# One ScalarE transfer per row of softmax sums, sums laid out by head, and another order in the last head pair

## The chip, the cores and the metric

The kernel runs on one core of a Trainium2 chip. A core has five engines with queues of their own, each strictly in order: TensorE (PE; its weight loads are shown as PEld), VectorE (DVE), ScalarE (ACT), GpSimd (POOL) and SyncE (SP), which only issues transfers here. Sixteen DMA engines carry out what SP, ACT and POOL issue. The metric is device time in microseconds (us) of one execution, lower is better.

## The reference, cut to what matters

One layer (sequence 1024, width 1024) runs two branches on the same normed input, a Mamba-2 scan and a forgetting attention with 16 heads of 64, and merges them by gates. The change touches the attention branch alone:

```python
for blk in range(seqlen // ATT_BLOCK):
    s = einsum('bhqd,bhkd->bhqk', q[:, :, q0:q1], k[:, :, :q1]) * scale
    s = s + fcum[:, :, q0:q1, None] - fcum[:, :, None, :q1]
    s = where(kpos <= qpos, s, -inf)
    prob = softmax(s, axis=-1)
    outs.append(einsum('bhqk,bhkd->bhqd', prob, v[:, :, :q1]))
...
y_att = o * silu(z_att)
merged = sigmoid(g_ssm) * (y_ssm @ w_branch_ssm) + sigmoid(g_att) * (y_att @ w_branch_att)
out = merged @ w_out;  x = x + rmsnorm(out)
```

All data is float32. The kernel computes large matrix products as sums of products of rounded parts ("h" and "l" tiles), and by a block scheme with seven products (steps 1 to 7 of a `Pair`) over sums and differences of operand blocks.

## The kernel before, in words

**Two strands of work.** `Stream` is the list of all projection steps, each a (pair of output units, one of seven products). It is pumped in halves (`stream.half`), in between the work of the stage that runs beside it. First come the input projections, then with the scan beside them, then with the attention beside them; at the end the stream runs alone through the second branch product (`wba`) and the output product (`merged`).

**The attention stage** (L1288 to L1640) loops over m = 0 to 48. A head pair hp (two heads, side by side on 64 partitions each) takes six values of m, its groups g = 0 to 5 (`GROUPS`, L1310): two blocks of 128 queries against one half of the keys. The groups (7,6), (5,4) need both key halves; (3,2) and (1,0) need one. In a group, `scores` multiplies q by k, adds the forget sums on DVE with a running minimum (`ex`, `nm`, L1459), takes the exponential on ACT with its row sum (`ex`, `sm`, L1463); `turned` transposes the result on PE (`pt`) and copies it out (`p`, L1483 on ACT, L1481 on DVE); in the next value of m `weighted` multiplies by v (`av`, L1494).

**Sums.** A head pair has three rows of results, n = 0, 1, 2, each 512 numbers wide per head, which end after g = 1, 3 and 5 (`end`). For n = 0 and 1 a row holds both key halves h of 256 queries; for n = 2 it holds the four blocks of g = 4 and 5. `settle` finds the common minimum of the two halves and exp of the differences; `scale` makes the factors `ns` (128 queries x 8); `send` turns them on PE into 8 rows x 128 (`tp`), copies them on ACT (`st`, L1385) and writes them to DRAM (`st_dram`, L1387, POOL, two transfers of 4 rows). `take` reads them back spread over 64 partitions per head (`rb`, L1393, two transfers on SP), and `out` multiplies the unnormed result by them (L1424 or L1418, DVE), adds the two halves (`zr`, L1425), and hands the row on through `outputs`.

**Order in one m.** Products of the former group; `free` (result times gate, L1412); scores; `stream.release()`; `settle` of the row that ends here; `take` (or, for rows 1 and 2 of the last head pair, `out`) of the row that ended at m - 2; some halves of the stream; `scale`; loads for later groups; `turned`; `out` at m - 2; `send` of the row that ended at m - 1; more halves. At the end of each m the stream's work on operand pieces is held back (`hold`), and `release` lets it go: `Operands.some` fetches pieces of the next branch product's operands (SP, L265) and splits pieces that have landed (ACT L277/L280, then DVE L278/L281, tiles x0 to x6).

**The last head pair.** For hp = 7 the finished rows don't go through DRAM: `out(1)` (at m = 47) makes with L1526 and L1527 the last pieces of the operands -t2 (x4), t3 (x5) and -b22 (x2), and `out(2)` (at m = 48) those of b21 (x1) and t4 (x6), through `put` and `direct`. The stream's step in the attention's last stretch, (wba 0, 6), reads -t2; steps 7 (t3), 1 of the next pair, 2 (b21), 4 (t4) and 3 (-b22) follow.

**What sets the order on an engine.** A planner sorts each engine's instructions by readiness in its own simulated time and by program order; `pin` ties an instruction behind the one written just before it on the same engine, and `high_priority` moves one forward. All matrix products, the transposes, the score work and the splits are pinned; `rb` loads, piece fetches and `settle`/`scale` aren't. The send's transfer is pinned, on POOL behind POOL's last instruction.

Of the kernel before, what the change touches and what calls it, by code (L numbers as in the profile page):

```python
# [12 lines left out]
ALU = mybir.AluOpType  # L13
# [3 lines left out]
P = 128  # L17
# [69 lines left out]
def hybrid_layer(ctx: ExitStack, tc, a, out):  # L87

    nc = tc.nc
# [42 lines left out]
    def turn(out_, in_, idn=ident):  # L132
        return tc.keep_in_program_order(nc.tensor.transpose(out_, in_, idn))  # L133

    def pin(op):
        return tc.keep_in_program_order(op)
# [1151 lines left out]
    with tc.tile_pool(name="att", bufs=1, reuse_waits="tile", side="right") as ap, tc.tile_pool(  # L1288
# [45 lines left out]
        class Heads:  # L1334
# [10 lines left out]
            def at(self, t, i, h, e):  # L1345

                if i < 4:
                    return t[2][:, i // 2, e, i % 2 : i % 2 + 1]
                return t[(7 - i) // 2][:, h, e, i % 2 : i % 2 + 1]

            def settle(self, n):

                if n == 2:
                    return
                nr = ap.tile([P, 2, 2], F32, tag="nr", name="nr")
                dd = self.dd[n] = ap.tile([P, 2, 2, 2], F32, tag="dd", name="dd")
                nm = self.nm[n]
                nc.vector.tensor_tensor(nr, nm[:, 0], nm[:, 1], ALU.min)
                for h in range(2):
                    nc.vector.tensor_tensor(dd[:, h], nr, nm[:, h], ALU.subtract)  # L1360
                nc.scalar.activation(dd, dd, AF.Exp)

            def scale(self, n):

                sm = self.sm[n]
                ns = self.ns[n] = ap.tile([P, 2, 2, 2], F32, tag="ns", name="ns")
                if n == 2:
                    nc.vector.reciprocal(sm, sm)
                    nc.vector.tensor_scalar(ns, sm, 0.5, None, ALU.mult)
                    return  # L1370
                dd = self.dd[n]
                nc.vector.tensor_tensor(sm, sm, dd, ALU.mult)
                nc.vector.tensor_tensor(sm[:, 0], sm[:, 0], sm[:, 1], ALU.add)
                nc.vector.reciprocal(sm[:, 0], sm[:, 0])
                flat = [x.rearrange("p h e t -> p h (e t)") for x in (ns, dd, sm)]
                over = flat[2][:, 0:1, :].to_broadcast([P, 2, 4])
                nc.vector.scalar_tensor_tensor(flat[0], flat[1], 0.5, over, ALU.mult, ALU.mult)

            def send(self, n):

                tp = pp.tile([P, HALF], F32, tag="s", bufs=4, name="tp")
                turn(tp[0:8, 0:P], self.ns[n].rearrange("p h e t -> p (h e t)"))
                st = small("st")[0:8, 0:P]
                with tc.high_priority():
                    nc.scalar.activation(st, tp[0:8, 0:P], AF.Copy)  # L1385
                for h in range(2):
                    pin(nc.gpsimd.dma_start(st_dram[self.hp, n, :, 256 * h : 256 * h + 256], st[4 * h : 4 * h + 4, :]))  # L1387

            def take(self, n):

# [181 lines left out]
        def end(m):  # L1572

            hp, g = divmod(m, 6)
            if 0 <= hp < NK and g % 2:
                yield heads[hp], g // 2
# [15 lines left out]
        def fill(m, part):  # L1592
            share = weights[min(m // 6, NK - 1)] * rooms[m % 6][part]
            to = stream.steps.index((ends[4], 6))
            stream.halves(round((2 * (to - stream.at) - (stream.run is not None)) * share / left[0]))
            left[0] -= share

        made = []
        for m in range(6 * NK + 1):

            for one in made:
                weighted(*one)
            for hd, which in end(m - 1):
                hd.free(which)
            if m == 6 * NK:
                stream.release()
                heads[NK - 1].out(2)
                break
            hp, g = divmod(m, 6)
            if not g:  # L1610
                heads[hp] = Heads(hp)
            for u in range(2):
                scores(hp, g, u)
            stream.release()
            for hd, which in end(m):
                hd.settle(which)
            for hd, which in end(m - 2):
                if not hd.last or not which:
                    hd.take(which)
                else:  # L1620
                    hd.out(which)
            fill(m, 0)

            for hd, which in end(m):
                hd.scale(which)
                hd.load_gates(which)
            loads(m)
            made = turned(hp, g)
            for hd, which in end(m - 2):
                if not hd.last or not which:  # L1630
                    hd.out(which)
            for hd, which in end(m - 1):
                hd.send(which)
            if m == 6 * NK - 1:
                heads[hp].send(2)
            stream.hold()
            fill(m, 1)
            for hd, which in end(m if m == 6 * NK - 1 else m - 1):
                if hd.last and which:
                    hd.take(which)  # L1640
# [59 lines left out]
```

## Time and profile before

| | us |
|---|---|
| median of 3 runs | 1342.09 (1340.25 to 1342.15) |
| profiled execution | 1341.3 |
| its span, first to last instruction | 1339.6 |
| PE busy | 1277.4 (95%) |
| DVE busy | 1017.7 (76%) |
| ACT busy | 787.0 (59%) |
| POOL busy | 307.4 (23%) |
| attention stage in that span | about 720 to 1185 |
| mean granted clock of PE | 0.986 |

The profile gives each instruction its start, its length and the idle time of its engine before it, with the event that ended that idle time ("<-"). A line such as `L1424 ... o<-o,rb` names the line of the kernel, the tiles written and read, and `x16` the number of instructions. Stretches are in microseconds from the span's start. The granted clock is what PE was given in a stretch, as a share of full speed; matmul ends are modelled, so a busy PE may still run at half speed. DMA issues have the time in which the issuing engine's queue is held and, apart from it, the time to landing.

### The profile page before, as it was taken

Reading aid. Unit: us, or ns where it says so; the run is one execution under the profiler, and the core shown is the slowest. Engines: PE = TensorE matmul, PEld = TensorE weight load, DVE = VectorE, ACT = ScalarE, POOL = GpSimd, SP = SyncE. Lnnn points to the kernel's source line nnn. Section 1 sums busy time; section 2 is a strip of 40 time slices with the busy share of each in tenths; the row PEclk is TensorE's granted clock in tenths of the full one; section 3 lists DMA queues with packets and bytes.
Section 4 is the critical chain, followed back from the end, with each engine's and each line's share of the span. In section 5 each row is a group of like instructions: output and inputs, shape, how many; then the busy total and the mean of one; then the engine's idle time right before and its main releaser. Section 6 shows DMA issues by size and latency. Waiting matters only on the chain.

```text
span 1339.6 us, 21075 instructions
## 1 busy us (share of the span) xinstructions
PE 1277.4 (95%) x7070; PEld 995.5 (74%) x7070; DVE 1017.7 (76%) x1978; ACT 787.0 (59%) x1726; POOL 307.4 (23%) x311
## 2 busy tenths in 40 slices
PE   6899999999999999999999999999889998889997
PEld 4578878777887888878877777777567766568786
DVE  7878986886888888888676576667676667776875
ACT  7645665465665666576556665556665555543664
POOL 4000340013400340034001122231111213235152
PEclk9999999999999999999999999999899998989999
DMA  8133542545436543654374556576765567556933
GB/s 286 59 105 79 163 143 100 176 161 164 123 114 205 174 118 115 200 179 129 125 279 150 168 201 204 185 232 222 264 215 192 192 200 239 186 158 193 355 121 102
DMA packets 154668, 233.59 MB, mean 174 GB/s; under 512 B 17216, under 2 KB 62656, under 8 KB 154560
## 3 DMA queue, kind: packets, MB, share of 16 engines
q1 hardware_dynamic: 142016, 205.53, 47.9%
q0 software_dynamic: 6400, 16.10, 3.2%
q10 hardware_dynamic: 6144, 10.62, 2.1%
q8 instruction: 55, 0.90, 0.3%
q14 instruction: 53, 0.43, 0.1%
HBM read 162.99 MB, written 72.34 MB: 176 GB/s over the span
## 4 chain that ended last, share of the span: by engine, by line
PE 60%; DMA 13%; DVE 11%; ACT 9%; issue 4%; SPq 1%; POOL 1%; ACTq 0%; DVEq 0%; POOLq 0%
PE pb L130 26%; PE pc L130 15%; PE pd L130 5%; PE av L130 3%; PE s L130 3%; ACT ex L1463 3%; PE pt L133 2%; PE yps L130 2%; DVE wop L352 2%; DVE ex L1459 1%; DMA raw<-in_wu 1%; ACT wop L351 1%; DMA st_dram<-st 1%; DMA rb<-st_dram 1%; PE tr L133 1%
## 5 line engine op out<-in xcount | busy, mean ns | idle before, releaser
L1463 ACT ACTIVATE ex<-ex,nm 128x512 f32<-128x512 f32 (+1 forms) x192 | 116.0, 606 | 149.7 <-DVE nm L1459 147.7
L352 DVE TENSOR_TENSOR wop<-sum,wop 128x512 fp32r<-128x512 f32 x180 | 139.2, 774 | 55.8 <-ACT wop L351 54.4
L351 ACT ACTIVATE wop<-sum 128x512 fp32r<-128x512 f32 x180 | 112.4, 625 | 81.6 <-DVE sum L357 30.3
L352 DVE TENSOR_TENSOR wop<-raw,wop 128x512 fp32r<-128x512 f32 x144 | 112.0, 779 | 45.2 <-ACT wop L351 41.6
L404 ACT ACTIVATE s<-pb 128x512 f32<-128x512 f32 x144 | 84.9, 590 | 89.6 <-PE pb L130 88.3
L130 PE MATMUL pc<-x3h,wop 128*128 128x512 f32 x384 | 132.2, 402 | 2.0 <-DVE th L418 1.2
L130 PE MATMUL pc<-x2h,wop 128*128 128x512 f32 x384 | 130.8, 399 | 3.0 <-DVE th L416 3.0
L130 PE MATMUL pb<-x4h,wop 128*128 128x512 f32 x384 | 130.4, 397 | 2.1 <-ACT x4h L277 2.1
L130 PE MATMUL pb<-x0h,wop 128*128 128x512 f32 x384 | 132.2, 401 | 0.0
L130 PE MATMUL pb<-x5h,wop 128*128 128x512 f32 x384 | 130.6, 399 | 1.5 <-ACT s L404 1.5
L130 PE MATMUL pb<-x6h,wop 128*128 128x512 f32 x384 | 130.0, 397 | 0.5 <-ACT s L404 0.5
L1459 DVE CUSTOM_DVE_ANT_0 ex<-s,fb 128x512 f32<-128x512 f32 (+1 forms) x192 | 95.7, 551 | 36.2 <-PE s L130 36.1
L133 PE MATMUL pt<-ident,ex 128*128 128x128 f32 x576 | 83.2, 287 | 16.4 <-ACT ex L1463 15.7
L130 PE MATMUL pd<-x1h,wop 128*128 128x512 f32 x288 | 96.6, 394 | 0.0
L351 ACT ACTIVATE wop<-raw 128x512 fp32r<-128x512 f32 x144 | 89.5, 622 | 11.7 <-PE pc L130 5.2
L133 PEld LDWEIGHTS pt<-ident,ex 128*128 128x128 f32 x576 | 69.2, 146 | 32.0 <-ACT ex L1463 25.7
L130 PEld LDWEIGHTS pc<-x3h,wop 128*128 128x128 f32 x384 | 73.1, 190 | 20.9 <-issue 2.6
L130 PEld LDWEIGHTS pc<-x2h,wop 128*128 128x128 f32 x384 | 72.1, 188 | 21.1 <-DVE th L416 4.3
L130 PEld LDWEIGHTS pb<-x5h,wop 128*128 128x128 f32 x384 | 73.1, 190 | 19.2 <-ACT s L404 2.7
L130 PEld LDWEIGHTS pb<-x4h,wop 128*128 128x128 f32 x384 | 72.3, 188 | 18.6 <-ACT x4h L277 2.5
L130 PEld LDWEIGHTS pb<-x0h,wop 128*128 128x128 f32 x384 | 73.3, 191 | 16.1 <-issue 0.7
L130 PEld LDWEIGHTS pb<-x6h,wop 128*128 128x128 f32 x384 | 72.7, 189 | 16.8 <-ACT s L404 0.9
(308 smaller groups left out, 2971.2 us busy)
## 6 DMA issues: line engine op xcount, KB each, us to landing
raw<-in_wu SPq DMA_DIRECT2D x128, 256.0 KB, 3.9
csb<-cs_dram SPq DMA_DIRECT2D x32, 256.0 KB, 5.3
fb<-f_dram SPq DMA_DIRECT2D x16, 512.0 KB, 6.6
rb<-st_dram SPq DMA_DIRECT2D x48, 128.0 KB, 3.0
wd<-in_wo SPq DMA_DIRECT2D x40, 128.0 KB, 3.0
xt<-in_x SPq DMA_DIRECT2D x8, 512.0 KB, 5.8
gs_dram<-th ACTq DMA_DIRECT2D x16, 256.0 KB, 3.5
qh_dram<-th SPq DMA_DIRECT2D x16, 256.0 KB, 2.9
```

The costliest lines, as they stand in the source:

```text
L130: return tc.keep_in_program_order(nc.tensor.matmul(*args, **kw))
L133: return tc.keep_in_program_order(nc.tensor.transpose(out_, in_, idn))
L351: nc.scalar.activation(op[:, 0], src, AF.Copy)
L352: nc.vector.tensor_tensor(op[:, 1], src, op[:, 0], ALU.subtract)
L404: nc.scalar.activation(s, ps, AF.Copy)
L1459: nc.vector.tensor_tensor_reduce(o, s[e][:, 0:w], fb[hp, h][:, e, 0:w], 1.0, 3.0e38, ALU.add, ALU.min, nm)
L1463: pin(nc.scalar.activation(o, o, AF.Exp, scale=-1.0, bias=nm, accum_out=hd.at(hd.sm, i, h, e)))
```

## The change

Three edits in the attention stage. (1) `send` issues one transfer of 8 rows from ScalarE's queue, right behind the copy it sends and moved forward by the planner with it, in place of two of 4 rows from GpSimd's. (2) So that the 8 rows lie in DRAM order (head, half, block), the tiles `nm`, `sm`, `dd` and `ns` are indexed head first, half second; the division in `scale`, one DVE instruction over both halves until now, becomes one for each half, since the sum over halves no longer broadcasts in one flattened operand. (3) In the loop, `take` (for the last head pair's rows 1 and 2 `out`) stands ahead of `stream.release()` and `settle`.

```diff
@@ class Heads
             def at(self, t, i, h, e):
                 if i < 4:
-                    return t[2][:, i // 2, e, i % 2 : i % 2 + 1]
-                return t[(7 - i) // 2][:, h, e, i % 2 : i % 2 + 1]
+                    return t[2][:, e, i // 2, i % 2 : i % 2 + 1]
+                return t[(7 - i) // 2][:, e, h, i % 2 : i % 2 + 1]
 ...
-                nc.vector.tensor_tensor(nr, nm[:, 0], nm[:, 1], ALU.min)
+                nc.vector.tensor_tensor(nr, nm[:, :, 0], nm[:, :, 1], ALU.min)
                 for h in range(2):
-                    nc.vector.tensor_tensor(dd[:, h], nr, nm[:, h], ALU.subtract)
+                    nc.vector.tensor_tensor(dd[:, :, h], nr, nm[:, :, h], ALU.subtract)
 ...
-                nc.vector.tensor_tensor(sm[:, 0], sm[:, 0], sm[:, 1], ALU.add)
-                nc.vector.reciprocal(sm[:, 0], sm[:, 0])
-                flat = [x.rearrange("p h e t -> p h (e t)") for x in (ns, dd, sm)]
-                over = flat[2][:, 0:1, :].to_broadcast([P, 2, 4])
-                nc.vector.scalar_tensor_tensor(flat[0], flat[1], 0.5, over, ALU.mult, ALU.mult)
+                total = sm[:, :, 0]
+                nc.vector.tensor_tensor(total, total, sm[:, :, 1], ALU.add)
+                nc.vector.reciprocal(total, total)
+                for h in range(2):
+                    nc.vector.scalar_tensor_tensor(ns[:, :, h], dd[:, :, h], 0.5, total, ALU.mult, ALU.mult)
 ...
-                turn(tp[0:8, 0:P], self.ns[n].rearrange("p h e t -> p (h e t)"))
+                turn(tp[0:8, 0:P], self.ns[n].rearrange("p e h t -> p (e h t)"))
                 st = small("st")[0:8, 0:P]
                 with tc.high_priority():
                     nc.scalar.activation(st, tp[0:8, 0:P], AF.Copy)
-                for h in range(2):
-                    pin(nc.gpsimd.dma_start(st_dram[self.hp, n, :, 256 * h : 256 * h + 256], st[4 * h : 4 * h + 4, :]))
+                    pin(nc.scalar.dma_start(st_dram[self.hp, n].rearrange("e (r c) -> (e r) c", r=4), st))
@@ the loop over m
             for u in range(2):
                 scores(hp, g, u)
-            stream.release()
-            for hd, which in end(m):
-                hd.settle(which)
             for hd, which in end(m - 2):
                 if not hd.last or not which:
                     hd.take(which)
                 else:
                     hd.out(which)
+            stream.release()
+            for hd, which in end(m):
+                hd.settle(which)
             fill(m, 0)
```

## The prediction

> **What bounds the kernel now.** I read the page first, then busy time by stretches, the waits, the chain of work around single sends, and the instructions in order of time at four places.
>
> ```profile
> span 1339.6 us, 21075 instructions
> ...
> 720.00:1185.00 465.00, 434.83 (x2864) 320.10 (x2861) 317.29 (x809) 276.29 (x711) 104.27 (x140) 0.97 0.63 206
> 959.67:963.08 3.41, 0.23 (x1) 0.14 (x1) 3.41 (x9) 0.95 (x4) 1.81 (x2) 1.00 0.24 50
> 963.08:969.91 6.83, 6.58 (x23) 4.12 (x24) 3.37 (x10) 4.39 (x13) 1.14 (x2) 0.50 0.76 257
> 1000.63:1004.04 3.41, 1.61 (x7) 0.73 (x5) 3.41 (x9) 1.77 (x5) 2.84 (x4) 1.00 0.99 308
> 1004.04:1010.87 6.83, 6.19 (x21) 4.67 (x23) 3.83 (x8) 3.18 (x9) 1.68 (x3) 0.50 0.52 193
> 1116.68:1120.09 3.41, 2.09 (x8) 0.98 (x6) 2.23 (x9) 2.65 (x8) 3.31 (x5) 1.00 0.88 299
> 1120.09:1126.92 6.83, 5.71 (x20) 4.50 (x22) 1.67 (x3) 2.96 (x8) 1.55 (x3) 0.50 0.63 204
> 1154.23:1157.64 3.41, 1.75 (x17) 1.06 (x16) 3.06 (x6) 3.10 (x7) 0.00 (x0) 1.00 0.84 262
> 1157.64:1161.05 3.41, 3.41 (x29) 2.44 (x28) 3.41 (x6) 0.00 (x0) 1.28 (x1) 1.00 0.33 114
> 1178.12:1181.53 3.41, 1.36 (x7) 0.81 (x5) 3.27 (x5) 0.71 (x2) 1.40 (x2) 1.00 0.28 41
> 1181.53:1188.36 6.83, 5.99 (x13) 3.91 (x14) 5.42 (x9) 4.18 (x8) 0.00 (x0) 0.50 0.89 287
> ```
>
> A stretch's columns are its length, then PE, PEld, DVE, ACT and POOL busy with instruction counts, the granted clock, the DMA share and GB/s. **TensorE is the bound**: in the attention stage (720 to 1185) it is busy 434.83 of 465, so only 30.2 us of idle time can come back directly. There is a second price. After the stretch at 959.67, in which PE worked 0.23 of 3.41 us, the clock is 0.50 for 6.83 us; likewise after 1.80 us of idle (1000.63), 1.32 (1116.68) and 2.05 (1178.12). After 1.66 us (1154.23) it stays at 1.00. So a stretch with some 1.3 to 1.8 us of idle can cost the next one half its speed: up to half of PE's 5.7 to 6.6 us there, some 3 us each. Short waits of PE are what this change can be worth, together with the clock they cost.
>
> The waits that the change aims at, and one send in full (the chain of waits):
>
> ```profile
> DVE o L1424 <- DMA rb<-st_dram: 7.3, 6, 2.3
> SPq L1393 <- DMA st_dram<-st: 101.8, 25, 8.3
> ...
> 989.91 0.15 ACT st L1385
> 990.34 0.54 POOL st_dram L1387
> 990.88 2.75 DMA st_dram<-st
> 994.27 3.15 DMA rb<-st_dram
> ...
> 997.51 0.69 DVE L1424 TENSOR_TENSOR o<-o,rb 128x512 f32<-128x512 f32 x1 [2.33 <-DMA rb<-st_dram]
> 954.87 0.69 DVE L1418 TENSOR_TENSOR zr<-o,rb 128x512 f32<-128x512 f32 x1 [1.89 <-DMA rb<-st_dram]
> 1154.58 0.69 DVE L1424 TENSOR_TENSOR o<-o,rb 128x512 f32<-128x512 f32 x1 [1.59 <-DMA rb<-st_dram]
> ```
>
> ACT copies the row of sums out (done at 990.06), POOL issues two transfers one behind the other, the second lands 2.75 us after its issue began, SP, which stood waiting for it, issues the broadcast `rb`, and DVE stands 2.33 us because its queue is in order and `o` is at its head. SP spends 101.8 us of the stage at this wait, but PE feels only what DVE passes on.
>
> **The change, part by part.** First the send (L1386 to L1387). The rows that price it:
>
> ```profile
> L1387 POOL DMA_DIRECT2D st_dram<-st x48: 547/572/584, 725.1 to 1177.1; - x48
> DMA to landing us min/median/max: 1.6/2.7/5.9
> L621 ACTq DMA_DIRECT2D gs_dram<-th x16: 326/327/355, 41.6 to 810.7; - x16
> 228.86 0.33 SPq L993 DMA_DIRECT2D rr_dram<-row  x1
> 230.57 0.81 SPq L996 DMA_DIRECT2D r<-rr_dram  x2
> 1148.21 0.72 ACT L1463 ACTIVATE ex<-ex,nm 128x512 f32<-128x512 f32 x1 [2.49 <-DVE nm L1459]
> ```
>
> Now the second transfer begins its issue 990.88 - 990.06 = 0.82 us after the copy ends. ScalarE issues behind its own instruction; I take that as immediate, so one issue of 0.33 us replaces a hop and two of 0.57. The landing itself I take as unchanged: the nearest transfer of the new shape, the 8 rows of 512 B that SP writes at 228.86, lets its reader go 1.71 us later, against 1.6 us for POOL's quietest. So **0.8 us earlier per send**. Bounds: nothing, where the write waits for other traffic (median 2.7 against 1.6) rather than for its issue; and 0.8 + (2.7 - 1.7) = 1.8 us if the single write also escapes that traffic.
>
> *The Trainium skill ("DMA: Bandwidth & Descriptors", Issuing engines are not separate DMA queues) says that transfers issued from another engine still run on the same 16 DMA engines and save only the time to initiate them. By that rule the 0.8 us is all there is, and the upper bound of 1.8 falls away; the 1.71 beside 1.6 us agrees.*
>
> What 0.8 us buys, place by place:
> - At 997.51 DVE starts 0.8 us earlier, PE's idle in the stretch at 1000.63 falls from 1.80 to 1.0. That is 0.8 us, and if the clock then holds, half of PE's 6.19 us, 3.1 more. An idle of 1.0 lies below every stretch quoted that lost the clock, but DVE's queue can refill it; I count the clock at 0.6. Term 2.7, ends 0 and 3.9.
> - At 954.87 DVE runs full through 963.08 (3.41 of 3.41), so 0.8 us comes through; PE still idles over 2 us, the clock falls anyway. Term 0.8, ends 0 and 1.8.
> - At 1154.58 the two issues stood behind another transfer on POOL, and PE's later pause is 1.48 us (row below). Term 1.0, ends 0 and 1.48.
> - The rest of the 7.3 us is in shorter waits. DVE has idle time elsewhere (317.29 busy of 465), so I give them no term.
>
> What it costs on ScalarE: 24 x 0.33 = 7.9 us. In its cover is the idle time in which ScalarE waits for the next scores: 2.49 us at 1148.21, the first instruction behind a copy `st` there. If that cover were gone, all 7.9 us would lie before `ex` and thus before PE's transposes. POOL is freed of 48 x 0.572 = 27 us; its remaining stores and differences come earlier, which I price at nothing.
>
> **Layout by head** (L1347 to L1377). Only the division is split:
>
> ```profile
> L1360 DVE TENSOR_TENSOR dd<-nr,nm 128x4 f32<-128x4 f32 x30 | 3.5, 158 | 0.4
> 1164.64 0.16 DVE L1377 SCALAR_TENSOR_TENSOR ns<-dd,sm 128x8 f32<-128x8 f32 x1
> 1167.70 0.27 PE L133 MATMUL tp<-ident,ns 128*8 128x128 f32 x1 [0.39 <-DVE p L1481]
> ```
>
> Sixteen instructions become 32 of four columns, by the first row 0.158 us each: at most 16 x 0.158 = 2.5 us more on DVE. `ns` is done 2.9 us before PE wants it even in the last pair, so only the length of DVE's queue counts, and only where DVE is full, as at 959.67. I charge 0.9 us for this and for the one or two places where ScalarE has no gap; ends 0 and 2.5 + 0.7.
>
> **The order at the start of a group** (L1614 to L1621). For every pair, SP's two `rb` loads now come ahead of the fetches of operand pieces that `release` emits, and the pieces' splits come ahead of `settle`. Queued behind SP's wait are then those pieces and the next q, k and v; the wait has been up to 8.3 us, but what stands behind the wait gets away when the row has landed, and that comes 0.8 us earlier than now. Term 0; the ends are a gain of 0.8 and, for pieces that went ahead until now, a loss of the wait itself, some 101.8 / 25 = 4 us of lateness, which PE feels only if its next step reads them. It bites in the last group (m = 47), where `out(1)` goes ahead of the splits:
>
> ```profile
> 1175.07 0.61 ACT L280 ACTIVATE x6h<-x6l 128x512 fp32r<-128x512 f32 x1
> 1175.59 0.57 ACT L1483 ACTIVATE p<-pt 128x512 f32<-128x512 f32 x1
> 1180.73 0.63 ACT L277 ACTIVATE x4h<-x 128x512 fp32r<-128x512 f32 x1 [4.41 <-DVE x L1526]
> ...
> 1175.10 0.68 DVE L278 SCALAR_TENSOR_TENSOR x2l<-x2l,x2h 128x512 fp32r<-128x512 f32 x1
> 1177.04 0.68 DVE L281 TENSOR_TENSOR x6l<-x6l,x6h 128x512 fp32r<-128x512 f32 x1
> 1180.01 0.68 DVE L1526 TENSOR_TENSOR x<-zr,x 128x512 f32<-128x512 f32 x1
> ...
> 1163.99 0.33 PE L133 MATMUL pt<-ident,ex 128*128 128x128 f32 x1 [1.48 <-ACT ex L1463]
> 1176.21 0.87 PE L130 MATMUL av<-p,v 128*64 128x256 f32 x8 [1.32 <-ACT p L1483]
> 1181.41 0.70 PE L130 MATMUL pb<-x4h,wop 128*128 128x512 f32 x1 [2.05 <-ACT x4h L277]
> ```
>
> PE stands 2.05 us for the last piece of -t2, which comes out of `out(1)` through `x`. Two splits (x2l, x6l) lie before `x` on DVE, 0.6 us apart each from the next instruction: without them `x4h` and PE's matmul come 1.2 us earlier. On ScalarE x6h no longer precedes `p`, 0.52 us off the 1.32. PE's idle in the stretch at 1178.12 then is about 2.05 - 1.2 + 0.5 = 1.35 us, between the cases that lost the clock and the one that kept it; I count half of 5.99, 3.0, at two thirds. Term 1.2 + 2.0 = 3.2, ends 0 (the planner or a late `rb` keeps `x` where it is) and 2.05 + 0.52 + 3.0 = 5.6. Late next are the moved pieces, x2 and x6; the steps that read them come after three others.
>
> **Sum**: 2.7 + 0.8 + 1.0 + 3.2 - 0.9 = 6.8 us. The profiled execution took 1341.3 us, 1.7 beyond its span; 1341.3 - 6.8 = 1334.5. The median of the runs shown, 1342.09, is 0.8 above it, so the forecast is **1335.3 us**.
>
> **The rivals.**
> - *Hidden anyway.* The 0.8 us per send disappears in traffic, and the planner, which orders what isn't pinned, shifts other DVE and ACT work so that pauses come up elsewhere. For: SP's 101.8 us shows that few of these waits reach PE; the clock fell after 1.32 us at 1116.68, a place that `rb` doesn't touch, and one new such place costs 1.3 + 2.9 = 4.2. Time: 1342.1 - 6.8 + 4.2 = 1339.5, and 1341.7 with half of the send's 4.5 us gone as well.
> - *Only the idle time returns.* The clock terms, 0.6 x 3.1 = 1.9 and 2.0, fail: PE's pauses shrink, but those stretches stay at 0.50, or others take their place. Time: 1335.3 + 3.9 = 1339.2. For it: 1.32 us lost the clock and 1.66 didn't, so a shorter pause is no warrant. *The Trainium skill ("TensorE: Matmul & The Clock Gate", What's actually happening) puts the half-rate state behind at least one idle window of about 3.4 us; by that rule no trimming of a 1.8 us pause wins clock, and the time would be this one. The trace differs: the stretch at 1000.63 had 1.61 us of matmuls in it and the clock fell all the same.*
> - *All pauses close.* Every term at its far end: 3.9 + 1.8 + 1.5 + 5.6 = 12.8, less 0.4: 1329.7; with the pause before 963.08 closed far enough to keep the clock (half of 6.58, 3.3) 1326. Against it: DVE is full at those places.
> - *Slower: ScalarE's queue stands.* ScalarE is in order, so when its transfer must wait for a free place behind an unrelated transfer, `ex` and `p` wait too, where POOL's wait held up nothing that PE needs. For it:
>
> ```profile
> ACT ex L1463 <- DMA ga_dram<-th: 1.9, 1, 1.9
> ```
>
>   one such wait of 1.9 us in this stage, on ScalarE. Against: it is one, and ScalarE issues gate transfers already (the row of 16 above). Price: the cover is about 2.5 us, so it decides where a wait passes 2.5 us or where a split or `p` follows at once. Three such places, each 1.9 us and one lost clock of 3, cost 8.7, against what is left of the gains in the tail, 3.2: 1342.1 + 5.5 = 1347.6.
>
> **How the numbers follow.** Forecast, 1329 to 1338: 0.41. Only idle, around 1339: 0.12. All closed, below 1329: 0.11. Hidden, within 2.7 us (0.2%, about what a measurement of this kernel can tell from no change) of 1342.1: 0.20. ScalarE's queue, above 1344.8: 0.16. So faster 0.64, same 0.20, slower 0.16. The range 1327 to 1346 leaves out some 0.06 below and 0.13 above.
>
> **What would show it.** Right: one ACT-queue issue of about 0.33 us per send and a transfer landing 1.6 to 3 us behind it; SP's wait for `st_dram` down by some 20 us; DVE's 7.3 us before `o` at less than half; the stretches after 1004 and 1181 at clock 1.00; PE's wait for `x4h` below 1.4 us. Wrong: ACT rows with waits for DMAs before `ex`; `x2l` and `x6l` still ahead of `x`; an unchanged or larger wait for `rb`; or new stretches at clock 0.50 in other pairs.

## The result, and the profile after

The changed kernel takes 1325.68 us (median of 7 runs, 1320.04 to 1333.79), the kernel before on the same chip 1340.25 (7 runs, 1336.59 to 1350.31): a ratio of **0.9887, 95% interval 0.9859 to 0.9914**, some 15 us less. The forecast was 1335.3. The runs of one kernel lie several us apart and go with the clock that PE was granted: of the changed kernel's seven, the one at 0.989 took 1333.79 us and the one at 0.995 took 1320.04.

The page of the changed kernel, its busy times, two of its queues (q0 is GpSimd's, q10 ScalarE's, by what the change moved) and the chain that ended last:

```profile
span 1325.7 us, 20994 instructions
...
PE 1268.7 (96%) x7070; PEld 990.7 (75%) x7070; DVE 1020.0 (77%) x1994; ACT 786.2 (59%) x1726; POOL 278.6 (21%) x263
...
q0 software_dynamic: 4864, 15.99, 3.2%
q10 hardware_dynamic: 6528, 10.72, 2.1%
...
PE 67%; DVE 10%; DMA 9%; ACT 9%; issue 3%; SPq 1%; POOL 1%; ACTq 0%; DVEq 0%; POOLq 0%
```

DVE, ACT and POOL changed by what was forecast: 16 more instructions on DVE, 48 fewer on POOL and 29 us less there. PE runs the same 7070 matmuls in the same order as before, so the two traces can be laid on each other matmul by matmul. How far the changed kernel is ahead at the start of a matmul, summed up by place (times of the kernel before):

```
stretch of the kernel before      us gained there   what PE's rows show
to 720, ahead of the stage        -2.4              +1.6 a clock fall at 55, -4.0 longer waits
720 to 900, short pauses          +3.0              up to 0.62 each before pt, tp and av, shorter or gone
937 pause for ex                  -0.8              0.93 -> 1.75
939 to 946                        -0.8              half clock for 6.8 us, was 3.4
963 pause for ex                  +2.5              3.88 -> 1.43
966 to 970                        +1.1              half clock for 3.4 us, was 6.8
970 to 1060, short pauses         +1.8              0.3 to 0.5 each before pt, gone
1003 pause for ex                 -1.4              1.38 -> 2.76
1004 to 1011                      +1.0              half clock for 3.4 us, was 6.8
1095 pause for p                  +1.3              1.45 -> 0.17
1119 to 1127                      +1.0              half clock for 3.4 us, was 6.8
1164 pause for ex                 +1.6              1.48 -> 0
1174 to 1181 tail, pauses         +2.2              tp 1.35 longer; av 1.32, x4h 2.05 gone
1181 to 1188 tail, clock          +3.0              half clock, now full
between these and behind          +0.8
sum                               13.9              spans 1339.6 and 1325.7
```

Ahead of 720 no instruction of the change runs, and the profiled executions of the experiments below lie between 3.4 us behind the kernel before and 2.2 ahead of it there, so the 2.4 us are what executions differ by. From 720 on the changed kernel gains 16.3 us: 5.3 are matmuls that ran at a better clock (1.1 + 1.0 + 1.0 + 3.0 - 0.8), and the other 11.0 are shorter pauses and what lies around them. The stage, and the stretches around the falls of the clock from 959 on, in the changed kernel (columns as before: length, PE, PEld, DVE, ACT, POOL busy, granted clock, DMA share, GB/s):

```profile
720.00:1185.00 465.00, 442.73 (x2946) 329.60 (x2943) 329.63 (x841) 282.14 (x722) 78.18 (x93) 0.98 0.63 210
...
959.20:962.61 3.41, 1.59 (x7) 0.73 (x5) 3.41 (x14) 1.89 (x8) 0.56 (x1) 1.00 0.65 163
962.61:969.44 6.83, 6.83 (x34) 4.72 (x35) 3.59 (x10) 4.04 (x10) 0.00 (x0) 0.75 0.76 239
1000.16:1003.57 3.41, 1.16 (x5) 0.59 (x6) 3.38 (x11) 3.06 (x9) 0.00 (x0) 1.00 0.63 235
1003.57:1010.40 6.83, 6.83 (x42) 5.37 (x43) 2.16 (x4) 1.81 (x5) 0.54 (x1) 0.75 0.21 74
1116.21:1123.04 6.83, 6.83 (x42) 5.19 (x41) 3.49 (x5) 2.57 (x6) 1.36 (x1) 0.75 0.50 157
1167.40:1170.80 3.40, 2.82 (x17) 2.08 (x18) 3.40 (x8) 2.25 (x6) 0.00 (x0) 1.00 0.01 1
1170.80:1177.60 6.80, 6.07 (x27) 4.71 (x26) 6.19 (x9) 4.03 (x8) 1.30 (x1) 1.00 0.74 243
```

The clock still falls after 962.61, 1003.57 and 1116.21, but the mean over 6.83 us is 0.75 where it was 0.50; in the tail it stays at 1.00. At 939 it went the other way: 0.50 over 6.82 us, where in the kernel before it came back after 3.41.

The waits of the changed kernel in the stage that the change aims at, and the same send as in the prediction:

```profile
SPq L1392 <- DMA st_dram<-st: 94.3, 21, 7.7
...
DVE o L1423 <- DMA rb<-st_dram: 4.2, 5, 2.0
...
986.72 0.25 ACT L1385 ACTIVATE st<-tp 8x128 f32<-8x128 f32 x1
987.00 0.29 ACTq L1386 DMA_DIRECT2D st_dram<-st  x1
988.29 1.59 SPq L1392 DMA_DIRECT2D rb<-st_dram  x2
994.08 0.69 DVE L1423 TENSOR_TENSOR o<-o,rb 128x512 f32<-128x512 f32 x1 [2.04 <-DMA rb<-st_dram]
```

From the end of the copy (986.97) to SP's `rb` it is 1.32 us; before it was 993.77 - 990.05 = 3.72. But `rb` itself now needs 5.79 us from its issue to DVE's start, against 3.74 before, so at this place nearly all of it was given back: DVE stands 2.04 us where it stood 2.33. Over all 24 sends, the mean from copy's end to SP's issue went from 4.15 to 2.76 us, and DVE stood 4.8 us in all before `o` or `zr`, against 10.8.

### The profile page after: what moved, and what is told of

Same layout as the page of the kernel before. It is cut to its first block, busy times and chain, and to the rows that moved or that the text cites. A ratio compares the mean times of both kernels' runs of the same rounds, so it can differ in the third digit from the quotient of the medians.

```text
span 1325.7 us, 20994 instructions
## 1 busy us (share of the span) xinstructions
PE 1268.7 (96%) x7070; PEld 990.7 (75%) x7070; DVE 1020.0 (77%) x1994; ACT 786.2 (59%) x1726; POOL 278.6 (21%) x263
## 3 DMA queue, kind: packets, MB, share of 16 engines
q0 software_dynamic: 4864, 15.99, 3.2%
## 4 chain that ended last, share of the span: by engine, by line
PE 67%; DVE 10%; DMA 9%; ACT 9%; issue 3%; SPq 1%; POOL 1%; ACTq 0%; DVEq 0%; POOLq 0%
PE pb L130 29%; PE pc L130 16%; PE pd L130 5%; PE av L130 4%; PE s L130 4%; PE pt L133 4%; ACT ex L1462 2%; PE yps L130 2%; DVE wop L352 2%; DMA raw<-in_wu 2%; ACT wop L351 1%; PE tr L133 1%; DMA xt<-in_x 1%; DVE ex L1458 1%; DVE sum L357 1%
## 5 line engine op out<-in xcount | busy, mean ns | idle before, releaser
L351 ACT ACTIVATE wop<-raw 128x512 fp32r<-128x512 f32 x144 | 89.5, 622 | 10.9 <-PE pc L130 5.0
L133 PE MATMUL pt<-ident,ex 128*128 128x128 f32 x576 | 80.4, 284 | 13.4 <-ACT ex L1462 13.0
```

Source lines behind the costliest of these rows:

```text
L351: nc.scalar.activation(op[:, 0], src, AF.Copy)
```

## The experiments

Two readings recur below, both from the profiled execution of each kernel: **L**, the mean over the 24 sends from the copy's end to the issue of `rb` on SP (4.15 before, 2.76 changed), and **D**, DVE's idle time ahead of the instructions `o` and `zr` that read `rb` (10.8 and 4.8). Ratios are to the kernel before on the same chip, with 95% intervals.

### The two halves of the change

The changed kernel with the old order in the loop (`send_only`), and the kernel before with only the new order (`order_only`):

```diff
 # send_only: the transfer and the layout of the change, but
             stream.release()
             for hd, which in end(m):
                 hd.settle(which)
             for hd, which in end(m - 2):   # take / out
 # order_only: L1387 and the layout of before, but
             for hd, which in end(m - 2):   # take / out
             stream.release()
             for hd, which in end(m):
                 hd.settle(which)
```

> The changed kernel with the loop's old order: one ScalarE transfer per row and the layout by head, but release and settle ahead of take and out. Theory A (the rows arrive earlier, everywhere): SP's rb loads follow the copy by some 2.8 us instead of 4.1, the gain is about 9 of the 15 us of the whole change, 0.6 to 0.7% under the kernel before, and the last group keeps its pause before x4h and a half-rate stretch after it. Theory B (the order in the last group gives nearly all): within 0.2% of the kernel before.

> The kernel before with the new order alone: take and out ahead of release and settle; two GpSimd transfers, old layout. Theory A: only the last group gains, 4 to 6 us (0.3 to 0.45%): PE's 2.05 us before x4h shrink to under 1.4 and the clock stays at 1.00 after it; TensorE's other pauses as before. Theory B: 12 us or more (0.9%).

`send_only` 0.9932 (0.9905 to 0.9958), L 2.64, D 1.5. `order_only` **1.0025 (1.0003 to 1.0046)**, L 4.14, D 12.8. The send alone brings most of the gain; the order alone, expected to bring 4 to 6 us, brings none. The execution profiled was its fastest (1335.39 us, median 1341.30), so the loss isn't in it, but its tail shows why nothing is won there, by DVE's and PE's instructions in order of time and two stretches:

```profile
1169.30 0.69 DVE L1424 TENSOR_TENSOR o<-o,rb 128x512 f32<-128x512 f32 x1 [0.15 <-DMA rb<-st_dram]
1169.91 0.16 DVE L1369 TENSOR_SCALAR ns<-sm 128x8 f32<-128x8 f32 x1
...
1171.85 2.11 DVE L1526 TENSOR_TENSOR x<-zr,x 128x512 f32<-128x512 f32 x1
...
1170.13 0.27 PE L133 MATMUL tp<-ident,ns 128*8 128x128 f32 x1 [0.62 <-DVE ns L1369]
1174.68 0.49 PE L130 MATMUL pb<-x4h,wop 128*128 128x512 f32 x1 [1.03 <-ACT x4h L277]
1175.82 0.50 PE L130 MATMUL pb<-x4l,wop 128*128 128x512 f32 x1 [0.65 <-DVE x4l L278]
1178.44 0.80 PE L130 MATMUL pb<-x5h,wop 128*128 128x512 f32 x1 [1.89 <-ACT s L404]
...
1173.83:1177.25 3.42, 1.23 (x3) 0.48 (x3) 3.33 (x7) 2.68 (x5) 0.10 (x1) 1.00 0.69 175
1177.25:1184.07 6.82, 5.62 (x13) 4.52 (x14) 4.90 (x8) 3.02 (x7) 0.00 (x0) 0.50 0.84 260
```

`o` stands ahead of `ns` (0.15 us of it for `rb`), but the planner has put `ns`, `p`, `wop`, `zr` and the split `x6l` ahead of `x`, which starts 5.33 us behind that group's first `ex` on DVE (1166.52), and PE's one pause of 2.05 us becomes four of 0.62, 1.03, 0.65 and 1.89, with the same half clock behind them. The same order in the changed kernel, DVE and ACT:

```profile
1163.69 0.42 DVE L1458 CUSTOM_DVE_ANT_0 ex<-s,fb 128x256 f32<-128x256 f32 x1 [2.28 <-PE s L130]
...
1165.96 0.69 DVE L1423 TENSOR_TENSOR o<-o,rb 128x512 f32<-128x512 f32 x1 [1.07 <-DMA rb<-st_dram]
1167.15 0.69 DVE L1525 TENSOR_TENSOR x<-zr,x 128x512 f32<-128x512 f32 x1
1167.76 0.16 DVE L1369 TENSOR_SCALAR ns<-sm 128x8 f32<-128x8 f32 x1
...
1167.87 0.63 ACT L277 ACTIVATE x4h<-x 128x512 fp32r<-128x512 f32 x1 [0.33 <-DVE x L1525]
```

In the changed kernel `x` is done 4.8 us ahead of where it was in the kernel before, counted from that group's first `ex` on DVE (1167.15 - 1163.69 = 3.46 us, against 1180.01 - 1171.73 = 8.28); only the `ns` of the last row is late, and PE waits 1.35 us for it.

### One transfer, two transfers, the layout

One transfer of 8 rows, but from GpSimd (`pool_one`), and two from GpSimd, one for each head, so that only the layout is new (`layout_two`); both in the old order:

```diff
 # pool_one
-                    pin(nc.scalar.dma_start(st_dram[self.hp, n].rearrange("e (r c) -> (e r) c", r=4), st))
+                pin(nc.gpsimd.dma_start(st_dram[self.hp, n].rearrange("e (r c) -> (e r) c", r=4), st))
 # layout_two
+                for e in range(2):
+                    pin(nc.gpsimd.dma_start(st_dram[self.hp, n, e].rearrange("(r c) -> r c", r=4), st[4 * e : 4 * e + 4, :]))
```

> Layout by head and one transfer of 8 rows per row of sums, but issued by GpSimd; the loop's old order. Theory C (one transfer in place of two is what counts, the issuing engine doesn't): as send_only, 0.6% or more under the kernel before. Theory A: it saves one issue of 0.57 us of the 1.3 to 1.4 us that ScalarE's transfer saves, so 0.2 to 0.35%.

> Layout by head alone, with its second division on DVE, and two GpSimd transfers of 4 rows, one per head; old order. All theories: DVE has 16 more instructions of about 0.16 us, 2.5 us in all, hidden where DVE has idle time: 0 to 0.2% above the kernel before. If it is well below, the layout or the new plan that comes with it has a worth of its own.

`pool_one` 0.9995 (0.9974 to 1.0017), L 3.55, D 10.6; `layout_two` 0.9997 (0.9975 to 1.0018), L 3.65, D 13.6. The layout costs and brings nothing that can be measured. One transfer for two does come earlier, 0.6 us on average, and brings nothing in this order, where 0.2 to 0.35% were expected. Next, the other corner: the layout of before and **two** transfers, but from ScalarE, in the new order (`act_two`), and the changed kernel a second time beside it:

```diff
 # act_two
-                for h in range(2):
-                    pin(nc.gpsimd.dma_start(st_dram[self.hp, n, :, 256 * h : 256 * h + 256], st[4 * h : 4 * h + 4, :]))
+                    for h in range(2):
+                        pin(nc.scalar.dma_start(st_dram[self.hp, n, :, 256 * h : 256 * h + 256], st[4 * h : 4 * h + 4, :]))
```

> The kernel before with two transfers per row, both from ScalarE's queue, old layout and one division, and the new order. Theory A: the second transfer leaves 0.33 us later than the one, so SP's rb loads follow the copy by about 1.6 us in quiet places instead of 1.3 (2.6 with GpSimd): 80% of the full gain, 0.8 to 1.1%. Theory C (number of transfers): nothing is gained, within 0.3% of the kernel before.

> The changed kernel once more, beside the three others on one chip. Theory A (ScalarE's queue takes 1.3 us off each row's way, and the order in the last group needs rows that early): 0.9 to 1.3% under the kernel before, as at first, and some 0.3 to 0.5% under the send alone.

`act_two` 0.9897 (0.9877 to 0.9917), `full_again` 0.9893 (0.9870 to 0.9916): with ScalarE as the issuer, two transfers do as well as one. The time from copy's end to `rb` at the six slow sends where DVE stood 0.7 us or more in the kernel before (head pair, row), beside the quickest send of all:

```
us         quickest  (0,1)  (1,1)  (3,2)  (4,1)  (5,0)  (7,0)    L     D    ratio
before       2.58     4.93   4.33   6.03   3.71   6.48   5.24   4.15  10.8  1
pool_one     1.90     4.90   4.30   5.52   3.36   6.25   4.04   3.55  10.6  0.9995
act_two      2.37     3.06   2.90   5.84   2.45   3.12   5.44   3.42   6.5  0.9897
changed      1.29     2.97   2.86   5.41   1.32   3.86   3.25   2.76   4.8  0.9887
```

GpSimd's one transfer saves 0.7 us where nothing is in its way and 0.03 to 1.2 at the six. ScalarE's two save 0.2 where nothing is in the way, 1.3 to 3.4 at four of the six, 0.2 at (3,2) and nothing at (7,0). Not all of that is traffic: at (5,0) GpSimd's own queue, standing for DVE's `th` ahead of another store, held the first issue back until 1.99 us behind the copy, where 0.29 is usual.

`pool_one` and `act_two` differ in the order, the layout and the number of transfers as well as in the engine. Three pairs differ in the engine alone: `pool_one` and `send_only` (0.9995 and 0.9932), `order_only` and `act_two` (1.0025 and 0.9897), and GpSimd's one transfer in the new order, which follows below, and the changed kernel (0.9948 and 0.9887). ScalarE is ahead by 0.6 to 1.3% in each. Its last issue begins 0.2 to 0.35 us sooner behind the copy, and from the start of that issue to `rb` the mean of the 24 sends is shorter: 2.60 us against 3.15, 2.65 against 3.18, 2.72 against 3.11. So the larger part of what ScalarE saves lies behind the issue. For one transfer 0.4 us of it is there at quiet sends too (1.26 against 1.67 at (7,1)); for two it is at busy sends alone.

### GpSimd's relief, and the place of `take`

GpSimd goes on writing the two transfers, into a tensor that nothing reads (`pool_held`); and only `out` of the last head pair is moved ahead, while `take` stays behind `release` and `settle` (`out_only`). Both are otherwise the changed kernel:

```diff
 # pool_held
+                for h in range(2):
+                    pin(nc.gpsimd.dma_start(spare[self.hp, n, h].rearrange("(r c) -> r c", r=4), st[4 * h : 4 * h + 4, :]))
 # out_only
             for hd, which in end(m - 2):
                 if hd.last and which:
                     hd.out(which)
             stream.release()
             for hd, which in end(m):
                 hd.settle(which)
             for hd, which in end(m - 2):
                 if not hd.last or not which:
                     hd.take(which)
```

> The changed kernel, and GpSimd besides writes the same two transfers of 4 rows to a spare tensor nobody reads, at the old place in its queue. Theory A (the way of the row counts): as the changed kernel, 0.8 to 1.3% under the one before. Theory D (what is gained is GpSimd's queue, which no longer stands 146 us for the copies and 27 us for its issues): back to within 0.3% of the kernel before.

> The changed kernel, but only the last head pair's out stands ahead of release and settle; take stays behind them as before. Theory A: as the changed kernel, within 0.2% of it, since take's place changes nothing where SP waits for the row anyway. Theory E (earlier rb loads on SP are the gain of the order): as the send alone, 0.6 to 0.75% under the kernel before.

`pool_held` 0.9873 (0.9852 to 0.9893), `out_only` 0.9881 (0.9864 to 0.9898): both have the whole gain. Neither the 27 us taken off GpSimd's queue nor the broadcast's place ahead of the piece fetches carries any of it that can be measured.

### Late rows from ScalarE

If the early rows are the cause, delaying them must take the gain away. The changed kernel with the copy written four times more ahead of the transfer (`act_late`):

```diff
                     nc.scalar.activation(st, tp[0:8, 0:P], AF.Copy)
+                    for _ in range(4):
+                        pin(nc.scalar.activation(st, tp[0:8, 0:P], AF.Copy))
                     pin(nc.scalar.dma_start(...))
```

> The changed kernel with the copy of the row repeated four more times on ScalarE ahead of its transfer, so that the transfer leaves some 0.6 us later; nothing else. Theory A (time on the row's way is what counts): quiet rows reach SP 1.9 us after the first copy, as with one GpSimd transfer, and a good part of the gain goes: 0.4 to 0.8% under the kernel before instead of 1.1%. Theory F (ScalarE's queue gets its transfer through traffic that holds GpSimd's, by more than the issue times; 0.6 us are small beside it): 0.85 to 1.1%.

0.9991 (0.9969 to 1.0013): the whole gain is gone. The delay was larger than meant, 1.66 us (the transfer leaves 1.70 us behind the first copy, 0.04 in the changed kernel), which makes L 4.18 and D 10.9, those of the kernel before. But the four copies are also 1.2 us of work on ScalarE ahead of `ex` and `p`, 24 times. So the same copies once more, **behind** the transfer and into columns that nothing reads (`act_load`), and half as many ahead of it (`act_late2`):

```diff
 # act_load
                     pin(nc.scalar.dma_start(...))
+                    for _ in range(4):
+                        pin(nc.scalar.activation(row[0:8, P : 2 * P], tp[0:8, 0:P], AF.Copy))
 # act_late2: as act_late, with range(2)
```

> The changed kernel with four more copies of a row on ScalarE written BEHIND the row's transfer, into columns that nothing reads: ScalarE's load is that of the kernel with four copies ahead of the transfer (some 1.4 us more for each of 24 rows), but the rows leave as early as in the changed kernel (mean from the copy's end to SP's broadcast 2.7 to 2.9 us, DVE before o and zr 4 to 6 us). Theory (the lateness of the rows cost the gain there): ratio 0.987 to 0.992, as the changed kernel. Rival (the 1.4 us of copies ahead of ex and p cost it, the rows being early or late no matter): 0.997 to 1.001, as the kernel with the copies ahead. In between, about 0.994: both have a part.

> The changed kernel with two more copies of a row ahead of its transfer instead of four: the transfer leaves some 0.8 us later than in the changed kernel, about as late on average as with one GpSimd transfer (mean from the copy's end to SP's broadcast 3.4 to 3.6 us). If the gain goes with the lateness step by step: half of it is left, ratio 0.993 to 0.996, as with one GpSimd transfer and the new order (0.9948). If any lateness at the places where DVE stands is enough: 0.998 to 1.000. If ScalarE's queue as such made the gain: 0.988 to 0.991.

`act_load` **0.9884 (0.9860 to 0.9907)**, with L 2.75, D 2.5: the load costs nothing that can be measured, so the lateness took the gain, with what the planner makes of it. `act_late2`, 0.82 us later than the changed kernel, has 0.9924 (0.9898 to 0.9950), L 3.43, D 9.9: about two thirds are left. The last rows but one of each, in order of time, first `act_late`, then `act_load`:

```profile
1168.12 0.25 ACT L1385 ACTIVATE st<-tp 8x128 f32<-8x128 f32 x1
1168.40 1.16 ACT L1387 ACTIVATE st<-tp 8x128 f32<-8x128 f32 x4
1169.59 0.27 ACTq L1388 DMA_DIRECT2D st_dram<-st  x1
1170.85 1.09 SPq L1394 DMA_DIRECT2D rb<-st_dram  x2
```

```profile
1161.99 0.25 ACT L1386 ACTIVATE st<-tp 8x128 f32<-8x128 f32 x1
1162.27 0.27 ACTq L1387 DMA_DIRECT2D st_dram<-st  x1
1162.59 1.16 ACT L1389 ACTIVATE st<-tp 8x128 f32<-8x128 f32 x4 [0.35 <-ACT st L1386]
1163.53 8.93 SPq L1395 DMA_DIRECT2D rb<-st_dram  x4
```

The same four copies of 1.16 us, ahead of the transfer in one and behind it in the other; SP goes 1.26 us after the transfer's issue in both, so 2.48 us behind the first copy's end in one and 1.29 in the other.

### The order, once the rows come a little earlier

`pool_one` with the new order (`pool_one_new`):

> One GpSimd transfer of 8 rows per row, layout by head, and the new order. Theory A: rows 0.6 us earlier than before are between, so the order in the last group gains a part: 0.2 to 0.5% under the kernel before. Theory F: GpSimd's rows still come late where DVE waits for them, so it stays within 0.25% of the kernel before.

0.9948 (0.9926 to 0.9970), against 0.9995 for the same transfer in the old order and 1.0025 for the new order with the old transfers. So the order is worth 0.5% here, 0.4% beside ScalarE's transfer (0.9887 to 0.9932, where the intervals overlap by a thousandth), and costs 0.25% when the rows come as late as before: the two parts of the change need each other. And in the new order GpSimd's one transfer in place of two is worth 0.8% (1.0025 to 0.9948), although it brought nothing in the old.

L and D hardly show where `pool_one_new` has its gain (3.51 and 11.5, as in `pool_one`). The matmuls do: the profiled executions of all these kernels have the same 7070 in the same order, and can be laid on the kernel before as above. Beside the gains stand the time from copy's end to `rb` of row (7,1), which `out(1)` needs in the tail, and how long behind the last group's first `ex` its `x` starts on DVE (8.28 us in the kernel before):

```
us              row (7,1)   x behind ex   gained 720 to 1174   gained in the tail, 1174 to 1200
old order
pool_one          1.96         6.91             -2.0                  0.9
layout_two        1.89         6.91              1.1                  3.3
send_only         1.29         6.85              9.9                  1.1
new order
order_only        2.58         5.33              3.0                 -0.2
act_late          2.49         5.53             -1.1                  2.0
act_two           2.41         4.59              5.4                  2.9
pool_one_new      1.96         3.02              1.9                  5.2
act_late2         1.88         4.57              6.2                  4.0
changed           1.29         3.46             10.5                  5.3
full_again        1.29         3.79             11.8                  3.4
pool_held         1.29         3.52             10.9                  5.2
out_only          1.31         3.64             10.2                  5.1
act_load          1.29         3.75              8.5                  4.8
```

These are single executions: two of the changed kernel are 2 us apart in the tail, `layout_two` lies as high in the old order (its 1.89 us is for the first head alone, whose `rb` waits for one of its two transfers), and `act_two`'s was the slowest of its six runs. Still, two parts come apart. Ahead of the tail 8.5 us and more are gained only where one ScalarE transfer leaves at once, in either order. In the tail the new order gains 3.4 to 5.3 us where row (7,1) takes less than 2 us, and 2.9 or less where it takes more. There the planner decides: in `order_only` and `act_late` it sets `ns`, `p`, `wop`, `zr` and `x6l` between `o` and `x`, in `pool_one_new` and the changed kernel `zr` and the reciprocal alone. A quiet send's 0.6 us was worth some 5 us there, by the order that came with it.

### Two tries for more

In the tail PE now waits 1.35 us for `ns`, which stands behind `o`. `ns_first` writes the last row's `scale` ahead of that `out`; `later_out` also writes `out` of the other rows behind the next `send`:

```diff
 # ns_first
+            for hd, which in end(m):
+                if hd.last and which == 2:
+                    hd.scale(which)
             for hd, which in end(m - 2):   # take / out
 # later_out, beside it
+            for hd, which in end(m - 1):
+                hd.send(which)
             for hd, which in end(m - 2):   # out
-            for hd, which in end(m - 1):
-                hd.send(which)
```

> The changed kernel, with the factors of the last row (reciprocal and product on DVE) written ahead of the last pair's out, since out now stands ahead of them in DVE's queue and PE waits 1.35 us for ns in the last group. The pause should shrink to about 0.3 us: 1 us (0.08%) below the changed kernel, not to be told from it; a look at whether the order has one more step to give.

> As ns_first, and for all rows that go through DRAM the products with rb are written behind the next row's send, so that DVE meets them later. Theory A: DVE's remaining 4.8 us in front of o and zr go to under 2 us, and with the pause of 2.8 us behind the one at 994 and its half-rate stretch 3 to 6 us come back: 0.2 to 0.45% below the changed kernel. Rival: what follows from the rows (gates' products, stores, pieces) comes later in turn, and the time is within 0.2% of the changed kernel or above.

`ns_first` 0.9914 (0.9882 to 0.9946), `later_out` 0.9907 (0.9871 to 0.9942): neither beats the changed kernel, and the intervals hold both a small loss and no difference. In both traces PE no longer waits for that `ns`, but the planner now sets `p`, `wop` and `x6l` as well ahead of `x`, which starts 5.16 us behind the group's first `ex` and no longer 3.46. In `later_out` D is 4.4, where under 2 was expected.

## Why the prediction was right in direction and wrong in size

Forecast 6.8 us, measured about 15 between medians and 13.6 between the profiled executions. Term by term, by the table of matmuls above:

**The send, "0.8 us earlier", was mis-sized: this is the step that failed.** It was worked out from issue times, and the landing was taken as unchanged because the nearest row (8 rows of 512 B written by SP) let its reader go after 1.71 us. ScalarE's transfer lets SP go 1.26 us after its issue; with nothing in the way SP starts 1.3 us earlier (2.58 to 1.29), on average 1.4. At the six busy sends of the table it is 0.6 to 2.6 us earlier. That is the bound "if the single write also escapes that traffic", which I had and did not take. *The Trainium skill ("DMA: Bandwidth & Descriptors", Issuing engines are not separate DMA queues) was the ground on which the prediction let that bound fall: the issuing engine saves only the time to initiate.* Here the measurement decides against it: with the issuing engine alone changed, the mean from the last issue's start to `rb` falls from 3.15 to 2.60 us (`pool_one`, `send_only`) and from 3.18 to 2.65 (`order_only`, `act_two`).

**"The rest of the 7.3 us is in shorter waits, no term" failed with it.** Short pauses before 900 and between 970 and 1060, and the one at 1095, gave 6.1 us, and shorter half-clock stretches at 966, 1004 and 1119 gave 3.1, less 0.8 for the longer one at 939; none of these had a term. The waits for `rb` left without one were no trifles: 0.74, 1.14 and 1.27 us at 754.20, 813.03 and 1037.45. DVE's wait for `rb` was the right row to look at, but it named only the head of an in-order queue; what stands behind it, such as the copies `p` that PE waits for at 1095, can come earlier too:

```profile
1089.77 0.44 PE L130 MATMUL av<-p,v 128*64 128x256 f32 x2 [0.17 <-DVE p L1480]
961.46 0.33 PE L133 MATMUL pt<-ident,ex 128*128 128x128 f32 x1 [1.43 <-ACT ex L1462]
1001.21 0.33 PE L133 MATMUL pt<-ident,ex 128*128 128x128 f32 x1 [2.76 <-ACT ex L1462]
```

**Place 997.51, 2.7 us: wrong in this execution.** The row left 2.4 us earlier and lost 2.05 of it in `rb`; PE's pause grew from 1.38 to 2.76 us and the clock fell (stretch from 1003.57). In the second run of the changed kernel DVE stood 0.22 us there and PE 0.94, so the place varies between executions; the prediction's bound of nothing stands for such a case.

**Places 954.87 and 1154.58, 0.8 and 1.0 us: the first is not shown, the second right in kind.** PE's pause behind 954.87 fell by 2.45 us (3.88 to 1.43), and "the clock falls anyway" held, for half the time. But row (3,2) left only 0.6 us earlier, and the gain at this pause is 1.9 to 2.9 us as well in `order_only`, `layout_two` and `act_late`, which gain nothing in all: the execution of the kernel before that was profiled had an unusually long pause there, and the agreement in kind is luck. The pause of 1.48 at 1164 is gone, 1.6 us. That one goes with the row: wherever one ScalarE transfer is sent at once, and in `act_late2`, 1.0 to 1.6 us are gained at it, and at most 0.4 in `pool_one`, `layout_two`, `order_only`, `pool_one_new`, `act_two` and `act_late`.

**The tail, 3.2 us, gave 5.2.** The mechanism held: `x` ahead of the splits, PE's wait for `x4h` gone, the clock kept. Two terms were small. `x` came 4.8 us earlier, not 1.2, because all of `out(1)` went ahead of `ns` and `p` and not only ahead of two splits; and the clock's 3.0 us, counted at two thirds, came whole. In the second execution (`full_again`) the clock did fall in the tail, for 3.4 us from 1169, and the tail gave 3.4. The pause that came instead was not foreseen as such:

```profile
1167.98 0.27 PE L133 MATMUL tp<-ident,ns 128*8 128x128 f32 x1 [1.35 <-DVE ns L1369]
1168.18 0.87 PE L130 MATMUL av<-p,v 128*64 128x256 f32 x8
1168.98 0.50 PE L130 MATMUL pb<-x4h,wop 128*128 128x512 f32 x1
```

This is the `ns` of the last row, (7,2), which now stands behind `o` and `x` on DVE; in the kernel before, its `tp` at 1174.62 had no pause ahead of it. The prediction looked at row (7,1) alone, whose `ns` it had 2.9 us early "even in the last pair".

**The order, "term 0" outside the tail, and 3.2 in it as a term of its own.** The prediction summed order and send; `order_only` shows that the order without the early rows loses 0.25%. The planner, which goes by its own time for the row, then leaves `x` 5.33 us behind `ex`. That condition, "a late `rb` keeps `x` where it is", stood there as the end 0, and the truth lay below it.

**Costs, 0.9 us: none seen.** ScalarE's issues took 0.27 to 0.52 us (median 0.29), no `ex` of the changed kernel waited for a transfer in this stage, and `act_load` put 1.2 us more on ScalarE behind each copy at no cost. The rival in which ScalarE's queue stands did not happen.

**Of the signs named ahead**, the 0.3 us issue, the tail's clock and the wait for `x4h` came out; SP's wait for `st_dram` fell by 7.5 us, not 20, and DVE's 7.3 became 4.2, not under half; the stretch behind 1004 stayed slow. "All pauses close", 1326 to 1329.7, is the rival that the time comes nearest to, although not all pauses closed: the gain came from more places than it counted. The range ended at 1327, below the sum of the far ends, although one cause, the mis-sized send, moves several of them at once.

**What stays open.** Why rows sent from ScalarE's queue reach their reader sooner behind the issue than rows from GpSimd's, and why (3,2) and (7,0) gained nothing with ScalarE's two. How much of a late row's cost is its arrival and how much the order that the planner makes of it: each kernel is planned anew, so `act_late` has both. How much of the gain is GpSimd's queue standing for other work, as at (5,0): `pool_held` shows only that its later work carries nothing. How the gain splits between pauses and clock in other executions than the profiled ones: with 5.3 of 16.3 us the clock has a large part, and runs of one kernel differ by as much. And the landing of ScalarE's transfers has no record, so it is read from SP's next issue.

## What to carry to other kernels

When a small transfer stands between two engines' work, price it by the time until its reader goes, at the places where something waits for it, and not by its issue alone: here GpSimd's one transfer, 0.6 us earlier on average, was worth nothing in the old order and 0.8% in the new, where the tail waited for the row. Where several terms of a sum hang on one estimate, let the range move them together. An instruction moved ahead in an in-order queue is a gain only if its own input is there by then, in the planner's time too; move the input first, and read the order that was made.

## What the runs showed of the hardware

- **The issuing queue matters behind the issue too.** Same rows, same destination: two transfers from ScalarE took 3.06, 2.90, 2.45 and 3.12 us from copy to reader at four busy sends where GpSimd's two took 4.93, 4.33, 3.71 and 6.48 (of which 1.7 in GpSimd's queue), but 5.84 and 5.44 at two others, against 6.03 and 5.24. Packets differ as well: two transfers took (6400 - 4864)/24 = 64 on GpSimd's queue q0, and (6432 - 6144)/24 = 12 on ScalarE's q10 (`act_two`). That this is the reason wasn't tried.
- **The granted clock can fall for half as long.** Behind idle times of 1.8 and 2.3 us in a 3.41 us stretch the clock was 0.75 over the next 6.83 us (962.61, 1003.57), where the kernel before had 0.50 behind 3.2 and 1.8. At 939 it was the changed kernel that had 0.50, behind 2.1 us, and the one before 0.75, behind 1.6. So the length of the fall doesn't go with the idle time ahead of it alone; what sets it isn't shown.
- **A load on ScalarE of 24 times 1.2 us was free** (`act_load`, 305.01 us busy of 465 in the stage against 282.14), although PE's remaining pauses for `ex` name ScalarE as the releaser:

```profile
720.00:1185.00 465.00, 441.95 (x2930) 327.50 (x2926) 327.20 (x839) 305.01 (x814) 77.35 (x93) 0.99 0.63 209
```
